# Shifted groups projected as one, and transposed q and k kept in tiles of four blocks

## The chip, the cores and the metric

The kernel runs on one core of a Trainium2 chip. The metric is the device time of one execution in microseconds; a time given for a kernel is the median of its runs.

## The reference, cut to what matters

One encoder block over 2048 tokens of 1024 channels. The input is normalised and projected once; of the projection, mixer A has 8 query heads over 2 heads of keys and values with a window of 128, and mixer B has three groups of 8 heads, each with its own window and dilation. In a dilated group the sequence falls into residue classes, and each class is a short sequence of its own with a window of 64 entries to both sides:

```python
B_GROUPS = ((128, 1), (512, 4), (2048, 16))
...
def dilated_group(q, k, v, window, dilation, bias_table):
    bsz, S, H, dh = q.shape
    L = S // dilation
...
    out, lse = banded_attention(to_sub(q), to_sub(k), to_sub(v), window // (2 * dilation),
                                dilation, bias_table, None)
```

Inside, q and k are normalised per head, logits get a bias by relative position, and everything outside of the window is masked. The three groups of B are then joined by their softmax denominators, both mixers are gated, projected, merged and projected again.

## The kernel before

**Units.** The attention is worked through in 14 units, `unit_order()`: two of A (4 query heads each) and twelve of B, two heads each, for four pairs of heads and three groups g. A unit of group 0 has one class of 16 blocks of 128 tokens, one of group 1 has 4 classes of 4 blocks, one of group 2 has 16 classes of one block. So every unit has 16 blocks, which it takes in eight pairs (`Pair`); 14 x 8 = 112 pairs are the clock of the schedule.

**Split numbers.** Activations and weights are kept as two 16-bit halves, `XH` and `XL`, `wh` and `wl`; a product is three matmuls (high by high, high by low, low by high) over 8 chunks of channels, 24 for a block, added up in one bank.

**Shifted units.** In groups 0 and 1 (`un.shift`) a query block of 128 needs 64 keys to both sides. So k and v of a block are projected from tokens shifted by 64 (`subset(..., aligned=False)`), while q is projected from the block as it stands. Block c of k and v then holds the last 64 tokens of block c-1 and the first 64 of block c; block 0 holds the last 64 of its class and the first 64. A query block reads two such blocks. `matmuls` (L642) writes 24 matmuls of 128 columns for q and 24 of 256 for k and v, into one bank `pj` of which there are two. Units of A and of group 2 have one run of 24 with 384 columns.

**From projection to transposed q and k.** `Pair.plan` places what follows by offsets from the moment a block's projection ends: `evac_qk` (L670) copies q and k to `rw` on ACT; `v_hi` (L685) and `v_lo` (L691) take v on ACT and DVE and so free the bank; then norms (`square`, `stats`, `newton`, `scale`, `gain`), the split into halves `spl` (`hi`, `lo`, `swap`), and `turn` (L741). `turn` issues one DMA transpose for each of the two blocks from SP, into a tile `kq` of its own, [128, 6, 128], of which there are six, or `kq0` for the first block of a shifted class, of which there are three (the last query block of a class needs that one again).

**Items.** A query block is an `Item`, in A one for each two heads. Its `plan` places logits (L792 on, matmuls at L803), maxima with bias (L818, DVE), exponentials (ACT), the split and the DMA transpose of the probabilities (L841, SP) and, some 1.8 pairs later, the product with the values (L852). Logits come three matmuls for each of its key blocks and head, 64 rows each, the two heads in the two halves of the array; each block has its own 128 (at the ends 64) columns of a bank `s`. There are three such banks and an item takes two. Items of a pair p come about 0.77 of a pair after that pair's `turn`.

**What sets the order.** Every step is put by `at(time, ...)` on a heap, and `until(time)` hands out what is due; the order on each engine is therefore written down by hand, and the times are in units of a pair. The projection's own matmuls are handed out evenly by their count: at the k-th of n the clock of the schedule stands at `pos + share * k / n`, and whatever is due then is put in between. The same stream has fills (`g_step`, `mg_step`: gate projections in matmuls of 512 columns, L308). Engines work in order, and SP is the one queue for all DMAs: weights, transposes, `z` out to memory and back, gates.

After the units come the gates, the branch products and the output product (L308, L1407, L1612), which the change doesn't touch.

Of the kernel before, what the change touches and what calls it, by code (L numbers as in the profile page):

```python
# [22 lines left out]
F16 = mybir.dt.float16  # L23
# [10 lines left out]
NCH = D // 128  # L34
# [67 lines left out]
T_OUT = (0.1, 0.1, 1.431, 2.0)  # L102
FILLS = ((2, None, (2, 2, 4, 5)), (3, 0, (8, 9, 10, 12)), (4, 1, (17, 18, 20, 21)), (5, 2, (24, 25, 26, 28)), (6, 3, (32, 35, 37, 38)), (7, 4, (40, 41, 42, 44)), (9, 6, (57, 59, 60, 61)), (10, 7, (64, 65, 66, 68)), (11, 10, (88, 89, 90, 92)), (8, 13, (116, 116, 118, 118)))
XT_BUFS = 14
KQ_BUFS = 6
VT_BUFS = 10
PT_BUFS = 4
N_BIAS_A = 384
# [3 lines left out]
def block_kernel(tc, x, w_units, w_gate, w_mrg, w_brn, w_out, w_bra, gain, qkg, sink, bias_a, bias_b, b_merge, out):  # L112
    nc = tc.nc
# [3 lines left out]
    T = nc.tensor  # L117
# [394 lines left out]
    def scale_time(t):  # L512
        return X_CH[0] + X_CH[1] * t
# [6 lines left out]
    for t in range(NT):  # L520
        b = X_SQ[0] + X_SQ[1] * t if t < 4 else X_SQ[2] + X_SQ[3] * (t - 4)
# [4 lines left out]
        b = scale_time(t)  # L526
        at(b, x_scale, t)
        for h in range(2):
            b = scale_time(t) + X_CH[2] + X_CH[5] * h
# [8 lines left out]
    for c in range(3):  # L538
        b = X_G[c]
# [34 lines left out]
    wk = main.enter_context(tc.tile_pool(name="wk", bufs=2, reuse_waits="tile"))  # L574
# [3 lines left out]
    def xclass(X, g, r):  # L578
        return X[:].rearrange("p c (j d) -> p c d j", d=DIL[g])[:, :, r, :]

    class Unit:


        def __init__(self, u):
            self.kind, self.idx, self.g = UNITS[u]
            self.u = u
            assert ("w", u) in done
            self.wh, self.wl = wtiles[u][3:5]
            if self.kind == "A":
                self.nq, self.nk, self.nv = 4, 1, 1  # L590
                self.d, self.n = 1, NT
            else:
                self.nq, self.nk, self.nv = 2, 2, 2
                self.d = DIL[self.g]
                self.n = S // self.d // 128
            self.br = 0 if self.kind == "A" else 1
            self.shift = self.kind == "B" and self.n > 1
            self.v, self.kq, self.t, self.done = {}, {}, {}, {}
            if self.kind == "A" or self.g == 0:
                self.nm = us.tile([128, NT, self.nq], F32, name=f"nm{self.kind}", bufs=2)  # L600

# [28 lines left out]
    def subset(X, g, r, c, aligned):  # L630
        o = 128 * c if aligned else (128 * c or S // DIL[g]) - 64
        return xclass((XH, XL)[X], g, r)[:, :, o:o + 128]

    class Pair:
# [7 lines left out]
        def matmuls(self, i):  # L642
            un, (r, c) = self.un, self.subsets[i]
            self.ps[i] = ps = pj_p.tile([128, 512], F32, name="pj")
            out = []
            for a, b, aligned in ((0, 128, True), (128, 384, False)) if un.shift else ((0, 384, True),):
                h, lo = subset(0, un.g, r, c, aligned), subset(1, un.g, r, c, aligned)
                k = 0
                for ch in range(NCH):
                    for lhs, rhs in ((h, un.wh), (h, un.wl), (lo, un.wh)):  # L650
                        out.append(lambda lhs=lhs, rhs=rhs, ch=ch, a=a, b=b, k=k: T.matmul(  # L651
                            ps[:, a:b], lhsT=lhs[:, ch, :], rhs=rhs[:, ch, a:b], start=(k == 0), stop=(k == 23)))
                        k += 1
            return out

        def plan(self, e):
# [82 lines left out]
                    G.tensor_copy(self.sp[:, i, :, 5, :], self.sp[:, i, :, 4, :])  # L739

        def turn(self):  # L741
            for i, s in enumerate(self.subsets):
                if self.un.shift and s[1] == 0:
                    kq = wk.tile([128, 6, 128], F16, name="kq0", bufs=3)
                else:
                    kq = wk.tile([128, 6, 128], F16, name="kq", bufs=KQ_BUFS)
                nc.sync.dma_start_transpose(out=kq[:, :self.nw, :], in_=self.sp[:, i].rearrange("p a b c -> p (a b c)"))
                self.un.kq[s] = kq


    class Item:
        def __init__(self, un, r, i, h0):
            self.un, self.r, self.i, self.h0 = un, r, i, h0
            n = un.n
            self.p0 = 0
            if un.kind == "A":
                cs = [c for c in (i - 1, i, i + 1) if 0 <= c < n]
                self.keys = [((0, c), 0, 128) for c in cs]
                self.b0 = 128 * (cs[0] - i + 1)
            elif n == 1:  # L760
                cs = [0]
                self.keys = [((r, 0), 0, 128)]
                self.b0 = 64
            else:
                cs = [i, (i + 1) % n]
                self.keys = [((r, i), 0 if i else 64, 128), ((r, (i + 1) % n), 0, 128 if i + 1 < n else 64)]
                self.b0 = self.p0 = 0 if i else 64
            self.segs = [(r, c) for c in cs]
            self.W = sum(b - a for _, a, b in self.keys)
            self.width = 128 * len(cs)  # L770

        def plan(self, s):
# [18 lines left out]

        def logits(self):  # L792
            un = self.un
            q = un.kq[(self.r, self.i)]
            self.sv = [s_p.tile([128, 512], F32, name="s")[:, :self.W] for _ in range(2)]
            nb = 3 if un.kind == "A" else 2
            o = 0
            for s, k0, k1 in self.keys:
                kt = un.kq[s]
                for i, (a, b) in enumerate(((0, 0), (0, 1), (1, 0))):  # L800
                    for j in range(2):
                        rows = slice(64 * j, 64 * j + 64)
                        T.matmul(self.sv[j][:, o:o + k1 - k0], lhsT=q[rows, nb * a + (self.h0 + j) // 2, :],  # L803
                                 rhs=kt[rows, nb * b + nb - 1, k0:k1], start=(i == 0), stop=(i == 2))
                o += k1 - k0

        def stat(self, j):
            un = self.un
# [251 lines left out]
    for u in range(NU + 1):  # L1060
        t = 8 * u
# [8 lines left out]
    for c, u, slots in FILLS:  # L1070
# [4 lines left out]
        t = 8 * u  # L1075
# [5 lines left out]
    for k in range(8):  # L1081
        u = 3 + k
        t = 8 * u
# [10 lines left out]
    un, nxt = None, 0.0  # L1094
    t = 0
    while t < NPAIR or heap or any(k >= t for k in fill):
        u, j = divmod(t, 8)
        steps = [(f, args) for f, *args in fill.pop(t, [])]
        if u < NU:
            if j == 0:  # L1100
                un = Unit(u)
# [341 lines left out]
    t = clock[0]  # L1443
# [120 lines left out]
    t = clock[0]  # L1564
# [7 lines left out]
    for k, (i, q) in enumerate(steps):  # L1572
# [3 lines left out]
        p = (i // 2, q % 2)  # L1576
# [168 lines left out]
```

## Time and profile before

| | us |
|---|---|
| median of 3 runs | 1980.72 (1979.74 to 1981.89) |
| the profiled execution | 1981.32 |
| its span, first to last instruction | 1979.5 |
| TensorE busy | 1963.7 |
| VectorE (DVE) busy | 1376.8 |
| ScalarE (ACT) busy | 1061.1 |
| GpSimd (POOL) busy | 875.6 |
| projection matmuls of the units, L651, first to last start | 79.9 to 1397.4 |

Busy times are the union of an engine's instructions. PE is TensorE, PEld its weight loads, SP the queue that issues DMAs; a line such as L651 is a line of the kernel. In rows of groups, "out<-in" are the program's tiles, then come partitions x elements of out and in, the count, and behind the bar the busy us and the mean ns of one. A PE row's end is modelled, so its start says more than its length. Rows of the timeline begin with the start in us and the length in us. Rows of windows give length, then for each engine busy us and count, the granted clock of TensorE, the share of the DMA engines and GB/s.

### The profile page before, as it was taken

Reading aid. Unit: us, or ns where it says so; the run is one execution under the profiler, and the core shown is the slowest. Engines: PE = TensorE matmul, PEld = TensorE weight load, DVE = VectorE, ACT = ScalarE, POOL = GpSimd, SP = SyncE. Lnnn points to the kernel's source line nnn. Section 1 sums busy time; section 2 is a strip of 40 time slices with the busy share of each in tenths; the row PEclk is TensorE's granted clock in tenths of the full one; section 3 lists DMA queues with packets and bytes.
Section 4 is the critical chain, followed back from the end, with each engine's and each line's share of the span. In section 5 each row is a group of like instructions: output and inputs, shape, how many; then the busy total and the mean of one; then the engine's idle time right before and its main releaser. Section 6 shows DMA issues by size and latency. Waiting matters only on the chain.

```text
span 1979.5 us, 49754 instructions
## 1 busy us (share of the span) xinstructions
PE 1963.7 (99%) x18614; PEld 1351.0 (68%) x18614; DVE 1376.8 (70%) x3604; ACT 1061.1 (54%) x2415; POOL 875.6 (44%) x2248
## 2 busy tenths in 40 slices
PE   8999999999999999999999999999999999999999
PEld 5557785677878888777888878888544444444444
DVE  6668776888767776667776778767867656776422
ACT  7457655766555566565566655656534545432200
POOL 4254445444445645446454565545520220232533
PEclk9999999999999999999999999999999999999999
DMA  6249976896848585466756675645731355788764
GB/s 248 80 86 171 186 141 142 141 187 129 172 82 176 105 167 114 104 135 149 134 128 131 122 148 118 132 102 102 163 98 55 118 175 182 219 241 271 251 222 153
DMA packets 540626, 295.98 MB, mean 150 GB/s; under 512 B 408928, under 2 KB 478176, under 8 KB 539104
## 3 DMA queue, kind: packets, MB, share of 16 engines
q1 hardware_dynamic: 540384, 292.81, 63.2%
q8 instruction: 145, 2.38, 0.5%
q14 instruction: 97, 0.79, 0.1%
HBM read 129.91 MB, written 65.27 MB: 99 GB/s over the span
## 4 chain that ended last, share of the span: by engine, by line
PE 93%; DVE 3%; POOL 2%; issue 1%; ACT 1%; DMA 0%; SPq 0%; DVEq 0%; POOLq 0%; ACTq 0%
PE pj L651 42%; PE pj L308 15%; PE fps L308 13%; PE fps L1612 7%; PE s L803 5%; PE fps L1407 5%; PE pv L852 4%; PE pt L914 1%; PE s L468 1%; POOL rs_t L270 0%; DMA xt<-in_x_dram 0%; DVE rw L717 0%; POOL rs_t L271 0%; POOL rs_t L272 0%; DVE qss L705 0%
## 5 line engine op out<-in xcount | busy, mean ns | idle before, releaser
L651 PE MATMUL pj<-wl,XH 128*128 128x128 f16 (+2 forms) x2816 | 717.7, 269 | 0.0
L651 PE MATMUL pj<-wh,XL 128*128 128x128 f16 (+2 forms) x2816 | 713.2, 269 | 0.0
L651 PE MATMUL pj<-wh,XH 128*128 128x128 f16 (+2 forms) x2816 | 708.6, 268 | 2.2 <-DVE vt L691 2.2
L651 PEld LDWEIGHTS <-XH 128*128 128x128 f16 x5632 | 575.3, 113 | 71.0 <-issue 2.6
L651 PEld LDWEIGHTS <-XL 128*128 128x128 f16 x2816 | 318.6, 113 | 37.8 <-issue 0.2
L270 POOL TENSOR_TENSOR rs_t<-rs_y 128x8 f32<-128x8 f32 (+2 forms) x345 | 101.2, 293 | 395.0 <-DVE rs_y L261 292.7
L818 DVE CUSTOM_DVE_ANT_0 pr<-s,b,ubuf 128x256 f32<-128x256 f32 (+3 forms) x512 | 219.2, 465 | 80.3 <-PE s L803 78.7
L835 DVE SCALAR_TENSOR_TENSOR p<-pr,p 128x512 f16<-128x512 f32 (+2 forms) x256 | 184.2, 720 | 24.7 <-ACT p L831 24.2
L670 ACT ACTIVATE rw<-pj 128x256 f32<-128x256 f32 (+1 forms) x224 | 86.9, 388 | 201.9 <-PE pj L651 199.8
L308 PEld LDWEIGHTS <-wh 128*128 128x128 f16 x960 | 93.7, 98 | 111.5 <-issue 1.4
L724 POOL TENSOR_TENSOR rw<-rw,g 128x128 f32<-128x128 f32 (+1 forms) x224 | 130.9, 603 | 85.9 <-DVE rw L717 53.3
L831 ACT ACTIVATE p<-pr 128x512 f16<-128x512 f32 (+2 forms) x256 | 159.5, 623 | 6.8
L308 PE MATMUL fps<-Y,wh 128*128 128x512 f16 x512 | 152.3, 379 | 0.0
L308 PE MATMUL pj<-XH,gh 128*128 128x512 f16 x384 | 146.0, 380 | 0.0
L308 PE MATMUL pj<-XH,gl 128*128 128x512 f16 x384 | 145.5, 379 | 0.0
L308 PE MATMUL pj<-XL,gh 128*128 128x512 f16 x384 | 145.5, 379 | 0.0
L1612 PE MATMUL fps<-wt,M 128*128 128x512 f16 (+1 forms) x684 | 145.2, 375 | 0.0
L717 DVE TENSOR_TENSOR rw<-rw,qr 128x512 f32<-128x512 f32 (+1 forms) x112 | 108.4, 968 | 50.1 <-POOL vt L678 33.7
L852 PEld LDWEIGHTS <-pt 128*128 128x128 f16 x3024 | 122.2, 97 | 22.1 <-DMA pt<-p 0.3
L180 POOL TENSOR_TENSOR wraw<-wraw,gn 128x768 f32<-128x768 f32 (+1 forms) x80 | 113.4, 1425 | 43.2 <-DMA wraw<-in_w_mrg_dram 29.5
L852 PE MATMUL pv<-vt,pt 128*128 128x65 f16 (+1 forms) x2784 | 131.7, 193 | 0.0
L803 PEld LDWEIGHTS <-kq 64*128 64x128 f16 x3024 | 82.9, 94 | 69.7 <-issue 65.8
(241 smaller groups left out, 3534.2 us busy)
## 6 DMA issues: line engine op xcount, KB each, us to landing
wraw<-in_w_units_dram SPq DMA_DIRECT2D x56, 384.0 KB, 4.7
mtd<-mm SPq DMA_DIRECT2D x56, 256.0 KB, 3.9
M<-mtd SPq DMA_DIRECT2D x8, 1792.0 KB, 9.0
mgd<-fg SPq DMA_DIRECT2D x39, 256.0 KB, 2.1
zd<-z SPq DMA_DIRECT2D x128, 66.0 KB, 1.8
zz<-zd SPq DMA_DIRECT2D x64, 132.0 KB, 2.8
xt<-in_x_dram SPq DMA_DIRECT2D x16, 512.0 KB, 8.6
gtd<-yo SPq DMA_DIRECT2D x32, 256.0 KB, 3.1
```

Of the source, the lines that this page charges most:

```text
L180: G.tensor_tensor(v, v, gn[:, c0:c0 + 2].unsqueeze(2).to_broadcast([128, 2, n]), OP.mult)
L270: G.tensor_tensor(tv, yv, yv, OP.mult)
L308: out.append(lambda w=w, xx=xx, ch=ch, i=i: T.matmul(ps[:], lhsT=w[:, ch, c0:c0 + 128], rhs=xx[:, ch, ts], start=(i == 0), stop=(i == n - 1)))
L651: out.append(lambda lhs=lhs, rhs=rhs, ch=ch, a=a, b=b, k=k: T.matmul(ps[:, a:b], lhsT=lhs[:, ch, :], rhs=rhs[:, ch, a:b], start=(k == 0), ...
L717: V.tensor_tensor(q, q, self.rr[:, :n].unsqueeze(2).to_broadcast([128, n, HD]), OP.mult)
L724: G.tensor_tensor(q[:, i, :un.nq, :], q[:, i, :un.nq, :], g, OP.mult)
L803: T.matmul(self.sv[j][:, o:o + k1 - k0], lhsT=q[rows, nb * a + (self.h0 + j) // 2, :], rhs=kt[rows, nb * b + nb - 1, k0:k1], start=(i == 0 ...
L818: V.tensor_tensor_reduce(out=self.pv[:, j, self.p0:self.p0 + W], in0=self.sv[j], in1=un.bias[:, self.h0 + j, self.b0:self.b0 + W], scale=I ...
L831: A.activation(self.sp[:, :128 * n], self.pr, AF.Copy, scale=PSC)
L835: V.scalar_tensor_tensor(self.sp[:, 128 * n:], self.pr, PSC, self.sp[:, :128 * n], OP.mult, OP.subtract)
L852: T.matmul(self.po[:, j, :w], lhsT=p[:, n * j + s, :], rhs=un.v[key][:, vh, c0:c0 + w], start=(k == 0 and s == 0), stop=(k == 2 and s == n ...
L1612: mm.append(lambda ch=ch, k=k, w=w, i=i: T.matmul(ps[:, :cols.stop - cols.start], lhsT=m[:, a, ch, k, :], rhs=wt[w][:, b, ch, cols], start ...
```

## The change

q of a shifted unit is projected from the shifted tokens too, together with k and v: one run of 24 matmuls with 384 columns. Transposed q and k then stand in tiles of 2048 columns, of which there are three. In a shifted unit a tile takes four blocks in the order of the tokens: four rows (`a`) of 512 columns, and block b of the shifted kind goes to columns 128 b - 64 to 128 b + 64. The block in which a tile begins is therefore transposed in two halves of 64 rows, one to the end of the tile before (or, for the first block of a class, to the end of the class's own tile) and one to the start of the new one. In group 0, whose class has four tiles, the first and last 64 tokens of the class that belong to query block 15 go to a small tile `kqe`, which takes a third transpose in the last pair. In units of A and of group 2 a tile takes the two blocks of a pair.

An item's q is then one stretch of 128 columns, and its keys are one or two stretches of 64, 128, 192 or 256 columns, as far as they lie side by side in one tile; each stretch is one set of three matmuls for each head.

```diff
 XT_BUFS = 14
-KQ_BUFS = 6
+KQ_BUFS = 3
 VT_BUFS = 10
...
             self.shift = self.kind == "B" and self.n > 1
-            self.v, self.kq, self.t, self.done = {}, {}, {}, {}
+            self.v, self.kq, self.kt, self.t = {}, {}, {}, {}
             if self.kind == "A" or self.g == 0:
...
             out = []
-            for a, b, aligned in ((0, 128, True), (128, 384, False)) if un.shift else ((0, 384, True),):
-                h, lo = subset(0, un.g, r, c, aligned), subset(1, un.g, r, c, aligned)
-                k = 0
-                for ch in range(NCH):
-                    for lhs, rhs in ((h, un.wh), (h, un.wl), (lo, un.wh)):
-                        out.append(lambda lhs=lhs, rhs=rhs, ch=ch, a=a, b=b, k=k: T.matmul(
-                            ps[:, a:b], lhsT=lhs[:, ch, :], rhs=rhs[:, ch, a:b], start=(k == 0), stop=(k == 23)))
-                        k += 1
+            h, lo = subset(0, un.g, r, c, not un.shift), subset(1, un.g, r, c, not un.shift)
+            k = 0
+            for ch in range(NCH):
+                for lhs, rhs in ((h, un.wh), (h, un.wl), (lo, un.wh)):
+                    out.append(lambda lhs=lhs, rhs=rhs, ch=ch, k=k: T.matmul(
+                        ps[:, :384], lhsT=lhs[:, ch, :], rhs=rhs[:, ch, :384], start=(k == 0), stop=(k == 23)))
+                    k += 1
             return out
...
         def turn(self):
-            for i, s in enumerate(self.subsets):
-                if self.un.shift and s[1] == 0:
-                    kq = wk.tile([128, 6, 128], F16, name="kq0", bufs=3)
+            un, nw = self.un, self.nw
+            def turned(out, i, rows=slice(0, 128)):
+                nc.sync.dma_start_transpose(out=out, in_=self.sp[rows, i].rearrange("p a b c -> p (a b c)"))
+            if not un.shift:
+                t = wk.tile([128, 2048], F16, name="kq", bufs=KQ_BUFS)[:, :256 * nw].rearrange("p (a b) -> p a b", a=nw)
+                for i, s in enumerate(self.subsets):
+                    turned(t[:, :, 128 * i:128 * i + 128], i)
+                    un.kq[s] = t, 128 * i
+                return
+            for i, (r, c) in enumerate(self.subsets):
+                m, b = divmod(un.n * r + c, 4)
+                if b == 0:
+                    un.kt[m] = wk.tile([128, 2048], F16, name="kq", bufs=KQ_BUFS)[:].rearrange("p (a b) -> p a b", a=4)
+                    if c == 0 and un.n > 4:
+                        un.ke = wk.tile([128, 4, 128], F16, name="kqe", bufs=1)
+                        turned(un.ke[:, :, 64:128], i, slice(0, 64))
+                    else:
+                        turned(un.kt[m if c == 0 else m - 1][:, :, 448:512], i, slice(0, 64))
+                    turned(un.kt[m][:, :, 0:64], i, slice(64, 128))
                 else:
-                    kq = wk.tile([128, 6, 128], F16, name="kq", bufs=KQ_BUFS)
-                nc.sync.dma_start_transpose(out=kq[:, :self.nw, :], in_=self.sp[:, i].rearrange("p a b c -> p (a b c)"))
-                self.un.kq[s] = kq
+                    turned(un.kt[m][:, :, 128 * b - 64:128 * b + 64], i)
+                if c == un.n - 1 and un.n > 4:
+                    turned(un.ke[:, :, 0:64], i, slice(64, 128))
 
...
                 cs = [c for c in (i - 1, i, i + 1) if 0 <= c < n]
-                self.keys = [((0, c), 0, 128) for c in cs]
+                self.W = 128 * len(cs)
                 self.b0 = 128 * (cs[0] - i + 1)
...
                 cs = [0]
-                self.keys = [((r, 0), 0, 128)]
+                self.W = 128
                 self.b0 = 64
...
                 cs = [i, (i + 1) % n]
-                self.keys = [((r, i), 0 if i else 64, 128), ((r, (i + 1) % n), 0, 128 if i + 1 < n else 64)]
+                self.W = 256 if 0 < i < n - 1 else 192
                 self.b0 = self.p0 = 0 if i else 64
             self.segs = [(r, c) for c in cs]
-            self.W = sum(b - a for _, a, b in self.keys)
             self.width = 128 * len(cs)
...
             un = self.un
-            q = un.kq[(self.r, self.i)]
+            q, keys = self.operands()
             self.sv = [s_p.tile([128, 512], F32, name="s")[:, :self.W] for _ in range(2)]
...
             o = 0
-            for s, k0, k1 in self.keys:
-                kt = un.kq[s]
+            for kt, k0, w in keys:
                 for i, (a, b) in enumerate(((0, 0), (0, 1), (1, 0))):
...
                         rows = slice(64 * j, 64 * j + 64)
-                        T.matmul(self.sv[j][:, o:o + k1 - k0], lhsT=q[rows, nb * a + (self.h0 + j) // 2, :],
-                                 rhs=kt[rows, nb * b + nb - 1, k0:k1], start=(i == 0), stop=(i == 2))
-                o += k1 - k0
+                        T.matmul(self.sv[j][:, o:o + w], lhsT=q[0][rows, nb * a + (self.h0 + j) // 2, q[1]:q[1] + 128],
+                                 rhs=kt[rows, nb * b + nb - 1, k0:k0 + w], start=(i == 0), stop=(i == 2))
+                o += w
+            assert o == self.W
+        def operands(self):
+            un, r, i, n = self.un, self.r, self.i, self.un.n
+            if not un.shift:
+                keys = []
+                for s in self.segs:
+                    t, o = un.kq[s]
+                    if keys and keys[-1][0] is t:
+                        keys[-1] = t, keys[-1][1], keys[-1][2] + 128
+                    else:
+                        keys.append((t, o, 128))
+                return un.kq[r, i], keys
+            m, b = divmod(n * r + i, 4)
+            t = un.kt[m]
+            q = (t, 128 * b) if i < 15 else (un.ke, 0)
+            if b == 0:
+                return q, ([(un.kt[m - 1], 448, 64)] if i else []) + [(t, 0, 192)]
+            if b < 3:
+                return q, [(t, 128 * b - 64, 256)]
+            if i == 15:
+                return q, [(t, 320, 128), (un.ke, 64, 64)]
+            return q, [(t, 320, 192)] + ([(un.kt[m + 1], 0, 64)] if i < n - 1 else [])
 
...
             un = self.un
```

## The prediction

> **What bounds the kernel now.** I read the page first: header, slices, chain.
>
> ```profile
> span 1979.5 us, 49754 instructions
> PE 1963.7 (99%) x18614; PEld 1351.0 (68%) x18614; DVE 1376.8 (70%) x3604; ACT 1061.1 (54%) x2415; POOL 875.6 (44%) x2248
> PE   8999999999999999999999999999999999999999
> ...
> PEclk9999999999999999999999999999999999999999
> ...
> PE 93%; DVE 3%; POOL 2%; issue 1%; ACT 1%; DMA 0%; SPq 0%; DVEq 0%; POOLq 0%; ACTq 0%
> ```
>
> TensorE is occupied in every slice, at the full granted clock, and 93% of the chain that ended last is its own work. DVE, ACT and POOL have a third or more of the span to spare. So whatever shortens TensorE's own stream shortens the run, as long as no other engine makes it wait. It hardly waits now, as the view of waits kept to TensorE says:
>
> ```profile
> PE pj L651 <- DVE vt L691: 2.2, 2, 1.8
> PE s L803 <- DVE nmB L818: 1.4, 1, 1.4
> ```
>
> (Columns: total us, times, longest us; the larger rows belong to the opening.) A busy TensorE isn't yet one that can go faster, because the durations of matmuls overlap. What counts is the distance from start to start, which the timeline shows. First the last stage, where one line runs unbroken (columns: start, us, instruction, count):
>
> ```profile
> 1839.67 40.52 PE L1612 MATMUL fps<-wt,M 128*128 128x512 f16 x187
> ...
> 1973.49 2.78 PE L1612 MATMUL fps<-wt,M 128*128 128x256 f16 x24
> ...
> L1612 PE MATMUL fps<-wt,M 128*128 128x512 f16 x660 | 142.6, 379 | 0.0
> ...
> L1612 PE MATMUL fps<-wt,M 128*128 128x256 f16 x24 | 2.8, 273 | 0.0
> ```
>
> The last two rows are of the groups by shape (busy us, mean ns of one): a matmul itself lasts 379 ns at 512 columns and 273 ns at 256. So 512 columns take (40.52 - 0.38)/186 = 215.8 ns from start to start, 256 take (2.78 - 0.27)/23 = 109.1 ns. The difference gives 0.417 ns a column, and what is left at no columns is 109.1 - 106.7 = **2.4 ns for each matmul, whatever its width**. By that line 128 columns should take 55.8 ns and 384 columns 162.5 ns. The line that the change edits agrees, in three unbroken stretches (24 rows of 128 and of 256, 29 of 384, first and next or last shown):
>
> ```profile
> 1201.44 0.22 PE L651 MATMUL pj<-wh,XH 128*128 128x128 f16 x1
> ...
> 1202.78 0.27 PE L651 MATMUL pj<-wh,XH 128*128 128x256 f16 x1
> ...
> 1208.11 0.27 PE L651 MATMUL pj<-wh,XH 128*128 128x256 f16 x1
> ...
> 1210.72 0.38 PE L308 MATMUL pj<-XH,gh 128*128 128x512 f16 x1
> ...
> 116.55 0.33 PE L651 MATMUL pj<-wh,XL 128*128 128x384 f16 x1
> ...
> 121.10 0.33 PE L651 MATMUL pj<-wh,XH 128*128 128x384 f16 x1
> ```
>
> 1.34/24 = 55.8 ns, 2.61/24 = 108.8 ns, 4.55/28 = 162.5 ns.
>
> **The change part by part.** *Projection of shifted groups.* Eight of the 14 units are shifted, 16 blocks each, 128 blocks. By shape, the groups of L651 are (one of three equal rows each, busy us and mean ns behind the bar):
>
> ```profile
> L651 PE MATMUL pj<-wh,XL 128*128 128x256 f16 x1024 | 280.9, 274 | 0.0
> ...
> L651 PE MATMUL pj<-wh,XL 128*128 128x384 f16 x768 | 252.5, 329 | 0.0
> L651 PE MATMUL pj<-wh,XL 128*128 128x128 f16 x1024 | 184.9, 220 | 0.0
> ```
>
> So 3 x 1024 = 3072 pairs (128 and 256 columns) become 3072 matmuls of 384. The columns stay; the fixed part goes once per pair: 3072 x 2.4 ns = 7.4 us. From the three stretches alone it is 55.8 + 108.8 - 162.5 = 2.1 ns, 6.5 us; with 109.1 for 256 it is 2.4. I take **-7.4**, bounds -6.5 and -8. That 3072 weight loads go too (113 ns each on the page) is worth nothing beyond this: at 55.8 ns from start to start they already lie beneath other matmuls.
>
> The Trainium skill speaks of the same spacing twice. TensorE: Matmul & The Clock Gate, under "Wait — 56ns, not 53.3ns?", has a fixed cost of about 2.5 ns per warm matmul, which by itself would make 7.7 us; the trace agrees with 2.4. The same page, under "Back-to-back issue gap", says that real streams of load and matmul sustain about 81 ns at 128 columns and 131 ns at 512; a straight line through these has 64 ns at no columns, and the sum would be 3072 x 64 ns = 197 us. The 55.8 and 215.8 ns above disagree with it.
>
> *Logits.* Keys that lie side by side in a tile go through in one matmul. From the code: in the 64 items of A six fewer each, in the 64 of group 1 six fewer, in group 0 nine of 16 items per unit have six fewer: 64x6 + 64x6 + 4x9x6 = 984 of 3024. Two heads run side by side, so 492 starts go. Rows of 18 and 12 such matmuls:
>
> ```profile
> 201.08 0.68 PE L803 MATMUL s<-kq 64*128 64x128 f16 x18
> ...
> 1140.85 0.51 PE L803 MATMUL s<-kq 64*128 64x128 f16 x12
> ```
>
> 0.17 us for three pairs of 128 columns is 57 ns a pair, the same 55.8 within the rounding. At 2.4 ns: **-1.2 us**, bounds 0 and -1.5. The number of times TensorE enters and leaves the 64-row form stays (256 items, each one group).
>
> *Transposes.* They are issued by SP:
>
> ```profile
> L747 SPq DMA_TRANSPOSE kq<-spl x224: 1188/1238/2262, 100.1 to 1416.2; - x112
> ...
>   PEld L803: 0.3, 1
> ...
> DMA to landing us min/median/max: 2.4/2.9/5.9
> ```
>
> Where a tile of four begins, the block is turned in two halves: one issue more in 16 classes of group 1 and 16 tiles of group 0, plus one at the end of each of four group 0 units: 36 more, 36 x 1.24 = 45 us of SP's time, beside TensorE. SP is in order: behind an extra issue wait the other k and q of the pair, the transposes of probabilities, z and weight loads. Half-height transposes into strided columns aren't in this trace; the nearest row bounds one at 1.19 us (the shortest issue) and 2.26 (the longest), and I take 1.24, as the issue time hardly depends on anything here. Only one load of logits ever waited for a landing (0.3 us), so there is slack; who has least of it? The logits that come first after a pair's turn:
>
> ```profile
> 1124.64 2.50 SPq L747 DMA_TRANSPOSE kq<-spl  x2
> DMA to landing us min/median/max: 2.5/2.8/3.1
> ...
> 1129.13 0.51 PE L803 MATMUL s<-kq 64*128 64x128 f16 x12
> ...
> 1404.07 2.50 SPq L747 DMA_TRANSPOSE kq<-spl  x2
> DMA to landing us min/median/max: 3.9/4.1/4.4
> ...
> 1408.85 0.34 PE L803 MATMUL s<-kq 64*128 64x128 f16 x6
> ```
>
> (The landing rows are those of the two issues above each.) In the third unit of group 0 the first of the pair landed 3.1 us after 1124.64 at the latest, 1.4 us ahead of 1129.13. In the last unit it landed by 4.4 us after 1404.07, 0.4 us ahead of 1408.85. Both are pairs at which a tile begins, so these logits now need the second issue, 1.24 us later. The first still has 0.1 to 0.2 us; the second is late by 0.9, and TensorE stands for it, with the fills queued behind.
>
> *Where logits stand between projections.* The interleaving counts matmuls. So far the first 24 of 48 were the short ones and took a third of a block's time; now time and count agree. A group written at half a block therefore comes up to a sixth of a block later, 24 x 162.5/6 = 0.65 us, in a shifted unit. At 1408.85 only fills are left, which stay as they are, and the up to four blocks between the pair's first eviction and these logits are shorter, 4 x 24 x 2.4 ns = 0.2 us, which makes the 0.9 above about **+1.1 us**. Later logits are later for DVE, whose maxima wait for them already, and behind these stand the evictions (L691) that free the projection's banks; those have a whole block, 3.9 us, so 0.65 us at the most is covered. Where that cover is gone, the two waits shown at the start are what it looks like. They came at one place:
>
> ```profile
> 1135.58 0.49 PE L803 MATMUL s<-kq 64*128 64x128 f16 x11 [1.36 <-DVE nmB L818]
> ...
> 1146.00:1154.00 8.00, 6.15 (x62) 5.13 (x60) 7.69 (x29) 4.65 (x14) 2.85 (x13) 0.79 0.84 186
> ```
>
> DVE was full there (7.69 of 8 us, third column of pairs) and the granted clock fell to a mean of 0.79 in the 8 us after the second wait, that is 8 x 0.21 = 1.7 us lost on top of 1.4 + 1.8: 4.9 us in all. The order on DVE isn't changed, so I leave it as it is: 0, bounds -4.9 (gone) and +4.9 (a second one like it).
>
> The Trainium skill speaks against the tiles: DMA: Bandwidth & Descriptors, in the row "DMA_TRANSPOSE effective BW", gives about 30% less where the middle dimension isn't contiguous, as now. By that the 2.9 us to landing would be 3.8 at most, the last unit would wait some 1.5 us more, and the sum would be -6.0. No row of this trace shows a strided one.
>
> *Sum.* -7.4 - 1.2 + 1.1 = **-7.5 us**. The profiled execution took 1981.3 us, 1.8 of it around its span of 1979.5; the median of the runs shown is 1980.7. From the median: 1973.2 us. Own range: -8.0 - 1.5 = -9.5, and -6.5 + 2.3 (the last unit late by 2.26 instead of 1.24, logits at nothing) = -4.2, so 1971.2 to 1976.5.
>
> **The rivals.** *The waits of DVE go as well.* Logits that come 0.2 us and more later give the second bank of scores more time. For it: one such place in a span. Against it: DVE, not TensorE, was late there. Time: 1973.2 - 4.9 = 1968.3.
>
> *DVE sets the pace in part.* Group 0 units have the merging of the three groups on DVE beside all else. If TensorE gained nothing in them (4 of 8 shifted units, 3.7 us) or one more stall of 4.9 us came: 1976.9 to 1978.1. For it: the full DVE above. Against it: 70% of the span.
>
> *The extra issues lie on the path (slower).* Place: the first logits after each of the 36 tiles' beginnings. Price: 1.24 us each, 44.6 us if all are late, 1980.7 - 8.6 + 44.6 = 2016.7. It decides from 8.6/1.24 = 7 of them being late in full. For it: two places have under 1.5 us. Against it: the 0.3 us in 3024 loads of logits.
>
> *Weight loads set the pace.* If every matmul had to last as long as its load of 113 ns, a pair cost 226 and one of 384 costs 162.5: 63 ns x 3072 = 195 us, 1785 us. The skill's 81 ns would give nearly the same. The row of 55.8 ns is against it.
>
> **How the numbers follow.** Runs of this kernel lie within 0.1% of each other; what it can tell from no change is about 0.2%, 4 us, so faster ends at 1976.8. Forecast 0.58; DVE's waits gone 0.14; DVE in part 0.18, two thirds of it above 1976.8; extra issues on the path 0.09, of which 0.05 beyond 1984.7 and 0.04 with a few late, within 0.2%; weight loads 0.01. Faster: 0.58 + 0.14 + 0.06 + 0.01 = 0.79. Same: 0.12 + 0.04 = 0.16. Slower: 0.05. The range takes in the rivals of DVE on both sides, 1968.3 and 1978.1, with a us beside each: 1967 to 1979.
>
> **What would show it.** L651's matmuls all at 384 columns, 5376, at 162.5 ns; L803's at 2040; its share of the time before 1400 shorter by 8 us, the last 500 us unchanged. Wrong: waits of TensorE for kq in more than two places; a longer row of waits for DVE in group 0; landings of kq far above 2.9 us; or the end of the projections (1397 us now) not some 7 us earlier.

## The result and the profile after

| | before | changed | ratio, 95% interval |
|---|---|---|---|
| median at first (7 runs each) | 1979.83 us | 1973.91 us | 0.9969, 0.9957 to 0.9980 |
| median once more (15 and 5 runs) | 1980.47 us | 1974.04 us | 0.9969, 0.9956 to 0.9981 |
| span of the profiled execution | 1979.5 us | 1971.7 us | |

Some 6 us by the medians (the ratio, 0.0031, is 6.1 us), 7.8 by the two spans; why these differ is seen below. The page of the changed kernel has, where the prediction showed these lines of before:

```profile
span 1971.7 us, 41743 instructions
PE 1952.1 (99%) x14558; PEld 1166.2 (59%) x14558; DVE 1374.9 (70%) x3604; ACT 1063.9 (54%) x2415; POOL 876.2 (44%) x2248
...
PE 90%; DVE 4%; POOL 2%; issue 1%; DMA 1%; ACT 1%; SPq 0%; DVEq 0%; POOLq 0%; ACTq 0%
```

The other engines do what they did, with the same counts; TensorE has 4056 matmuls fewer, 3072 of the projection and 984 of the logits, and is still what ends last. Its spacing at the edited line, in a shifted unit (first row of an unbroken stretch of 16, and what follows):

```profile
1200.12 0.33 PE L650 MATMUL pj<-wh,XL 128*128 128x384 f16 x1
...
1202.72 0.38 PE L308 MATMUL pj<-XH,gh 128*128 128x512 f16 x1
```

2.60/16 = 162.5 ns, as forecast for 384 columns. Where the time went, from two windows of each kernel, up to the end of the units' projections and after it (length first; then PE's busy time):

```profile
79.00:1397.50 1318.50, 1314.93 (x15348) 1039.78 (x15347) 968.74 (x2817) 798.16 (x1965) 681.87 (x2036) 1.00 0.68 134
1397.50:1979.50 582.00, 577.47 (x2862) 266.48 (x2859) 350.10 (x648) 208.99 (x357) 165.71 (x155) 1.00 0.58 181
```

```profile
79.00:1388.00 1309.00, 1304.18 (x11311) 855.02 (x11310) 968.13 (x2817) 801.19 (x1965) 681.70 (x2035) 1.00 0.65 135
1388.00:1971.70 583.70, 577.53 (x2843) 266.08 (x2841) 348.73 (x648) 208.77 (x358) 166.44 (x156) 1.00 0.58 181
```

The first stretch is 9.5 us shorter, the second 1.7 longer. TensorE's waits, from the view of waits of the changed kernel (total us, times, longest):

```profile
PE pj L650 <- DVE vt L690: 2.7, 2, 2.4
PE s L818 <- DVE nmB L857: 2.0, 1, 2.0
...
PE s L818 <- DMA kq<-spl: 0.7, 1, 0.7
PE pt L953 <- DVE ya L1054: 0.6, 1, 0.6
```

The two waits for DVE are those of before, 2.2 and 1.4 us then, each about half a us longer. The last two are new and lie in the second stretch: 1.3 of its 1.7 us. One more row is of the weight loads of the logits, where the kernel before had a single wait of 0.3 us:

```profile
PEld L818 <- DMA kq<-spl: 2.5, 5, 1.2
```

Five loads now waited for a transpose; only the longest of these waits held the matmuls up, by the 0.7 us above. The granted clock differs too. Around the wait for L690:

```profile
1139.50:1147.50 8.00, 5.63 (x39) 3.59 (x38) 7.72 (x28) 4.45 (x13) 2.62 (x13) 1.00 0.64 150
```

At this place the kernel before had a mean of 0.79 over 8 us. Here it is 1.00 although the wait was longer (the last section shows what decides this). So 1.7 of the 7.8 us between the spans are a stretch of half clock that one execution had and the other didn't.

### The profile page after: what moved, and what is told of

It is laid out like the page before. It is cut to its first block, busy times and chain, and to the rows that moved or that the text cites. A ratio compares the mean times of both kernels' runs of the same rounds, so it can differ in the third digit from the quotient of the medians.

```text
span 1971.7 us, 41743 instructions
## 1 busy us (share of the span) xinstructions
PE 1952.1 (99%) x14558; PEld 1166.2 (59%) x14558; DVE 1374.9 (70%) x3604; ACT 1063.9 (54%) x2415; POOL 876.2 (44%) x2248
## 4 chain that ended last, share of the span: by engine, by line
PE 90%; DVE 4%; POOL 2%; issue 1%; DMA 1%; ACT 1%; SPq 0%; DVEq 0%; POOLq 0%; ACTq 0%
PE pj L650 41%; PE pj L308 14%; PE fps L308 13%; PE fps L1651 7%; PE s L818 5%; PE fps L1446 5%; PE pv L891 4%; PE pt L953 1%; PE s L468 1%; POOL rs_t L270 1%; DVE rw L716 1%; POOL rs_t L271 0%; DMA xt<-in_x_dram 0%; DVE qss L704 0%; DVE p L874 0%
## 5 line engine op out<-in xcount | busy, mean ns | idle before, releaser
L650 PE MATMUL pj<-wl,XH 128*128 128x384 f16 x1792 | 589.6, 329 | 0.0
L650 PE MATMUL pj<-wh,XH 128*128 128x384 f16 x1792 | 584.6, 326 | 2.7 <-DVE vt L690 2.7
L650 PE MATMUL pj<-wh,XL 128*128 128x384 f16 x1792 | 586.4, 327 | 0.0
L650 PEld LDWEIGHTS <-XH 128*128 128x128 f16 x3584 | 412.0, 117 | 177.3 <-issue 23.6
L650 PEld LDWEIGHTS <-XL 128*128 128x128 f16 x1792 | 209.5, 117 | 69.4 <-issue 2.1
L818 PE MATMUL s<-kq 64*128 64x256 f16 (+2 forms) x1992 | 123.1, 242 | 2.7 <-DVE nmB L857 2.0
```

The lines of the kernel that those rows point to most:

```text
L650: out.append(lambda lhs=lhs, rhs=rhs, ch=ch, k=k: T.matmul(ps[:, :384], lhsT=lhs[:, ch, :], rhs=rhs[:, ch, :384], start=(k == 0), stop=(k ...
L818: T.matmul(self.sv[j][:, o:o + w], lhsT=q[0][rows, nb * a + (self.h0 + j) // 2, q[1]:q[1] + 128], rhs=kt[rows, nb * b + nb - 1, k0:k0 + w] ...
```

## The experiments

All are edits of the changed kernel, except the last.

**Two parts and three parts.** The projection alone, cut again, from the same shifted tokens:

```diff
-            k = 0
-            for ch in range(NCH):
...
-                        ps[:, :384], lhsT=lhs[:, ch, :], rhs=rhs[:, ch, :384], start=(k == 0), stop=(k == 23)))
+            for a, b in ((0, 128), (128, 384)) if un.shift else ((0, 384),):
+                k = 0
...
+                            ps[:, a:b], lhsT=lhs[:, ch, :], rhs=rhs[:, ch, a:b], start=(k == 0), stop=(k == 23)))
```

and with `((0, 128), (128, 256), (256, 384))`.

> The changed kernel with the projection of shifted blocks again in 24 matmuls of 128 columns and then 24 of 256, from the same shifted tokens; tiles, transposes and logits as changed. Theory A (each matmul has a fixed 2.4 ns, and 3072 fewer of them are the gain): 3072 x 2.4 = 7.4 us more, some 1 us of it swallowed where TensorE waits for DVE in the third unit of group 0: 1973.9 + 6.4 to 7.4 = 1980.3 to 1981.3. Rival B (the gain is in the logits, the tiles, or waits that moved): within 2 us of 1973.9.

> The same projection in three parts of 128 columns, 72 matmuls a block, 6144 more than changed. Theory A: 6144 x 2.4 = 14.7 us more, 1987 to 1989, twice the step of two parts; starts 55.8 ns apart. Rival C (weight loads set the pace below some width, 113 ns a load in the groups): 72 loads a block instead of 24, far more than twice the step of two parts, up to 6144 x 113 ns = 694 us.

Two parts: 1981.88 us, ratio to before 1.0006 (0.9996 to 1.0015), that is 0.0037 above the changed kernel's 0.9969, 7.3 us (the median itself lies above the range expected, as does the median of the kernel before beside it, 1981.05 us). Three parts: 1987.86 us, 1.0040 (1.0025 to 1.0055), 0.0071 or 14 us above it. So 3072 matmuls more cost 7.3 us and 6144 cost 14: 2.4 and 2.3 ns each. By the intervals these differences are good to about 3 and 4 us, an estimate, so the clock alone gives 2.4 ns only to within 1 ns; the starts below give it closer. In three parts (66 starts between the first and the last row):

```profile
1147.23 0.22 PE L651 MATMUL pj<-wh,XH 128*128 128x128 f16 x1
...
1150.91 0.22 PE L651 MATMUL pj<-wh,XH 128*128 128x128 f16 x1
```

3.68/66 = 55.8 ns with a weight load for each. Loads don't set the pace; rival C and the prediction's last rival are out. Two parts are as slow as the kernel before although their logits are the wide ones, so rival B is out as well.

**Keys by 128.**

```diff
+            keys = [(kt, k0 + i, min(128, w - i)) for kt, k0, w in keys for i in range(0, w, 128)]
             for kt, k0, w in keys:
```

> The changed kernel with its logits' keys cut into at most 128 columns again: 3024 matmuls for 2040. Theory A: 492 pairs x 2.4 ns = 1.2 us more, 1975.1; a group of 12 lasts 441 ns to the next matmul instead of 434 of 6 wide ones. Rival B (logits carry the gain): 1979 or more.

1976.94 us, 0.9981 (0.9972 to 0.9990): 0.0012 or 2.4 us above the changed kernel. The expectation miscounted: in 24 items of group 0 keys of 192 and 64 columns now become three pieces, not two, which makes 3168 matmuls for the logits. The count of all matmuls says so too, 1128 more than the changed kernel's 14558:

```profile
PE 1954.9 (99%) x15686; PEld 1186.0 (60%) x15686; DVE 1375.4 (70%) x3604; ACT 1064.4 (54%) x2415; POOL 877.7 (44%) x2248
```

That is 564 pairs, and theory A's price is 1.4 us; it lies within what the two intervals allow, and so does no difference at all. Rival B's 1979 isn't reached. The profiled execution also has a stretch of half clock (window; the granted clock is the third figure from the end) and waits 0.8 us longer for a transpose (view of waits):

```profile
1127.00:1135.00 8.00, 6.03 (x52) 3.30 (x51) 7.62 (x23) 5.73 (x15) 4.86 (x13) 0.79 0.86 199
```

```profile
PE s L819 <- DMA kq<-spl: 1.5, 1, 1.5
```

How much is due to the matmuls themselves shows in the starts. Changed kernel, a group of six with 256 columns and what follows; before, a group of twelve with 128:

```profile
1256.06 0.50 PE L818 MATMUL s<-kq 64*128 64x256 f16 x6
1256.49 0.38 PE L650 MATMUL pj<-wl,XH 128*128 128x384 f16 x1
```

```profile
1140.85 0.51 PE L803 MATMUL s<-kq 64*128 64x128 f16 x12
1141.29 0.28 PE L651 MATMUL pj<-wh,XL 128*128 128x256 f16 x1
```

0.43 against 0.44 us is at the rounding of the view, but the traces hold starts to 1 ns and there are many such groups. From a group's first start to the next projection matmul, in the mean of all that no wait interrupts: 434.0 ns for six wide ones (58 groups of the changed kernel) against 441.3 ns for twelve (58 groups with keys by 128); in A 601.3 against 608.8 ns (38 groups each). Each saves 7.3 to 7.5 ns for three pairs, 2.4 to 2.5 ns a pair. For 492 pairs that is the 1.2 us of the prediction, shown by the starts where the clock can't resolve it.

**More transposes.**

```diff
                 if b == 0:
+                    turned(wk.tile([128, 4, 64], F16, name="kqx", bufs=2)[:], i, slice(0, 64))
```

> The changed kernel with one half-height transpose more (into a tile that nobody reads) ahead of the others wherever a tile of four begins: 32 more issues of SP. Theory A (extra issues lie beside TensorE, but for the last unit): 32 x 1.24 = 40 us more of SP, the wait in the last unit longer by 1.2 us, one or two new ones of under 1 us each: 1975 to 1977. Rival P (extra issues lie on the path): 10 to 40 us more, 1984 to 2014.

1974.05 us, 0.9970 (0.9960 to 0.9980): no different from the changed kernel, and a us below what theory A forecast. Rival P's 10 us and more are out. The extra issues aren't free, though: with 32 more (first view, by line) TensorE's wait in the last unit is longer by 1.0 us in the profiled execution, and ten loads of logits wait, 5.0 us in all, for five and 2.5 us (view of waits). The other nine stay hidden.

```profile
L744 SPq DMA_TRANSPOSE kqx<-spl x32: 1169/1171/1686, 216.5 to 1395.3; - x32
```

```profile
PE s L819 <- DMA kq<-spl: 1.7, 1, 1.7
...
PEld L819 <- DMA kq<-spl: 5.0, 10, 2.2
```

**The wide part first.** Two parts in the order `((128, 384), (0, 128))`.

> The two-part projection with its order turned round: 24 matmuls of 256 columns (k and v) and then 24 of 128 (q). As many matmuls as with the narrow part first; only the place of logits and values between the projections moves, which is at 0.77 of a block by count: at 0.70 of its time with the narrow part first, at 0.77 undivided, at 0.85 here. Theory A (the count of matmuls is what costs, the place doesn't): the same as the two-part kernel within 1.5 us, ratio to before 1.000 to 1.002. Rival D (the place of logits made the gain or a loss): 2 us or more away from it.

1981.73 us, 1.0009 (0.9999 to 1.0018), the two-part kernel's within 0.6 us. Where logits stand between the projections is worth nothing that shows here; the two intervals together leave room for some 2.5 us, so rival D's 2 us aren't seen, though not shut out to the last us.

**The preparation of a gate chunk.** Both waits for DVE lie in the third unit of group 0. In the changed kernel, DVE's short operations ahead of the maxima there, and POOL beside them (timelines):

```profile
1126.82 0.41 DVE L1029 TENSOR_TENSOR bm_n<-zz 128x4 f32<-128x4 f32 x1
1127.26 0.97 DVE L1030 TENSOR_TENSOR bm_n<-bm_n,zz 128x4 f32<-128x4 f32 x1
1128.26 1.02 DVE L1031 TENSOR_TENSOR bm_e<-bm_n,zz 128x12 f32<-128x12 f32 x1
1129.20 0.47 DVE L857 CUSTOM_DVE_ANT_0 pr<-s,b,ubuf 128x256 f32<-128x256 f32 x1
...
1127.17 1.03 POOL L324 TENSOR_TENSOR wraw<-wraw,gn 128x512 f32<-128x512 f32 x1
1128.15 0.10 POOL L677 MEMSET vt<- 128x2 f16 x1
1128.20 1.03 POOL L324 TENSOR_TENSOR wraw<-wraw,gn 128x512 f32<-128x512 f32 x1
```

4 columns take DVE 0.97 us and end when POOL's operation ends. L324 belongs to the weights of gate chunk 11, which this unit prepares.

```diff
-(11, 10, (88, 89, 90, 92))
+(11, 9, (88, 89, 90, 92))
```

> The changed kernel with the weights of one gate chunk (fill 11: gain L324 on POOL, square, split L354 on DVE) prepared one unit earlier, in the group 2 unit ahead of the third group 0 unit; its fills stay where they are. Theory E (TensorE waits there for DVE because this preparation falls into it: POOL's gain of 1.03 us twice beside DVE's short operations, which take 0.97 and 1.02 us instead of 0.17, and L354's 1.28 us ahead of an eviction): waits for L857 and L690 of 2.0 and 2.4 us go, 4 to 5 us less, 1969 to 1970. Rival F (DVE is too full in a group 0 unit without fills, whatever is prepared): the waits stay within 1 us, 1973 to 1974.

> The changed kernel once more, beside the two that follow: 5 to 8 us below the kernel before (ratio 0.996 to 0.9975).

> The kernel with the preparation of chunk 11 moved one unit ahead, once more. Theory E: 3 to 5 us below the changed kernel of this call, ratio to before 0.994 to 0.9955.

At first 1970.34 us, 0.9953 (0.9938 to 0.9968); once more, beside the changed kernel's repetition, 1970.44 us, 0.9951 (0.9937 to 0.9964) against 0.9969 (0.9956 to 0.9981). That is 3.6 us below the changed kernel by the medians, and the best version here. DVE's operations and TensorE's waits in the second run:

```profile
1127.19 0.17 DVE L1030 TENSOR_TENSOR bm_n<-bm_n,zz 128x4 f32<-128x4 f32 x1
1127.39 0.18 DVE L1031 TENSOR_TENSOR bm_e<-bm_n,zz 128x12 f32<-128x12 f32 x1
```

```profile
PE pj L650 <- DVE vt L690: 1.6, 2, 1.2
...
PE s L818 <- DVE nmB L857: 0.5, 1, 0.5
```

0.17 and 0.18 us, and 1.6 + 0.5 of waiting instead of 2.7 + 2.0. Theory E has the cause of a little over half of the waits, 2.6 us, and the gain of 3.6 us stays short of the 4 to 5 it forecast; the other waits stay with the unit. The edit takes POOL's gain and DVE's own L354 out of the unit together, so their shares aren't separated.

**Fills in that unit, and later logits.**

```diff
-(11, 10, (88, 89, 90, 92))
+(11, 9, (82, 84, 85, 87))
...
-                nxt = max(nxt, t + LS)
+                nxt = max(nxt, t + LS + (.2 if u == NU - 1 else 0))
```

> As the kernel before it in this call, and the four fills of this chunk go into the third group 0 unit (pairs 82, 84, 85, 87) instead of the next unit, so that TensorE has 5.2 us more to do in four of its pairs. Theory E: nothing more to win, 1969 to 1970. Rival F: only now the waits go, 4 us or more below the kernel before it.

> As the one before, and the logits of the last unit are placed 0.2 of a pair (1.6 us) later. If the wait for the second half of a transposed block in the last unit (0.7 us in the changed kernel) is worth its length, 0.7 us less; waits for kq gone. If the later logits only push the end of the unit, 0 to 2 us more.

Both miss. With the fills moved: 1980.61 us, 1.0004 (0.9995 to 1.0014), 10 us above the kernel without. The unit that lost the fills now waits for DVE (in the last row, the longer of the two; the shorter is the changed kernel's):

```profile
PE s L818 <- DVE nmB L857: 4.0, 2, 3.7
PE s L818 <- DVE z L857: 1.9, 1, 1.9
PE pt L953 <- DVE ya L1054: 1.6, 2, 1.1
```

With later logits in the last unit too: 1989.23 us, 1.0049 (1.0034 to 1.0064). The wait for kq is gone, as forecast, but the waits for DVE grew, four for the maxima and two for L690, where the run before had two and one (of 0.3 us). What these two rows grew by, 3.6 us, lies in the last unit; the rest of the 9 us isn't traced here:

```profile
PE s L818 <- DVE nmB L857: 5.6, 4, 3.7
PE pj L650 <- DVE vt L690: 2.3, 2, 2.0
```

**The kernel before, with the preparation moved.** The edit of `FILLS` above, on the kernel before.

> The kernel before with the same preparation moved one unit ahead: the undivided change is then measured on a schedule with less waiting for DVE. Theory E: its waits for L818 and L691 in the third group 0 unit (1.4 and 1.8 us) shrink by 2 us or more and with them the stretch of half clock that followed: 2 to 4 us below before, 1976 to 1978. Theory A: the step from it to the kernel of 384 columns with the same move is 7 to 8 us, a little more than the step between the two unmoved kernels, as less of it goes to DVE. Rival: the step is the same or smaller.

1977.36 us, 0.9988 (0.9979 to 0.9996). Its wait for L691 is 1.2 us in all and that for the maxima's bank is gone, as theory E has it. From it to the best version the ratio falls by 0.0037, 7.3 us; between the unmoved two it falls by 0.0031, 6.1 us. That is theory A's direction, but the intervals overlap, so whether the change gives back a us to DVE's waits stays open by the clock; only the waits themselves show it (3.6 us before, 4.7 after; with the preparation moved 1.2 and 2.1).

## Why the prediction was right

1973.2 us was forecast, 1973.9 measured, and the mechanism is the one forecast. That the number is so close is in part luck: the forecast starts from the median of three runs, 1980.7, where that of seven is 1979.8. The step was to be 7.5 us and is 6.1 by the ratio. The spans say 7.8, but with the 1.7 of half clock, 6.1 again. The terms as they came out add up to it: -7.4 for the projection, -1.2 for the logits, +0.7 for a transpose, +1.1 for the two old waits for DVE, +0.6 for a new one (L1054) = -6.2 us.

- **Projection, -7.4.** Right in mechanism and size: 162.5 ns at 384 columns, and 7.3 us between the two-part kernel and the changed one.
- **Logits, -1.2.** Right by the starts, 7.3 to 7.5 ns a group; by the clock only consistent.
- **Transposes, +1.1.** A wait of 0.7 us in the last unit, but not the one that was worked out. In the pair that was named the first landings now took 3.0 us at most where they had taken 4.4, and its logits (1399.92) didn't wait. The wait came one pair later, for a transpose of full height:

```profile
1395.14 3.77 SPq L744 DMA_TRANSPOSE kq<-spl  x3
...
1399.92 0.51 PE L818 MATMUL s<-kq 64*128 64x192 f16 x12
...
1403.62 0.44 SPq L175 DMA_DIRECT2D wraw<-in_w_mrg_dram  x1
1404.17 1.76 SPq L880 DMA_TRANSPOSE pt<-p  x1
1406.08 3.26 SPq L744 DMA_TRANSPOSE kq<-spl  x2
...
1411.16 0.50 PE L818 MATMUL s<-kq 64*128 64x256 f16 x6 [0.73 <-DMA kq<-spl]
```

  The landings of these three and of these two `kq` issues (view of the line, each in its window), and below them those of the same last two in the kernel before:

```profile
DMA to landing us min/median/max: 2.4/2.5/3.0
...
DMA to landing us min/median/max: 4.0/4.5/5.0
```

```profile
DMA to landing us min/median/max: 2.5/2.6/2.7
```

  So the cause is a landing of 5.0 us. The issue in halves may still stand behind it. In the kernel before the same issues of SP are:

```profile
1404.07 2.50 SPq L747 DMA_TRANSPOSE kq<-spl  x2
...
1411.68 0.48 SPq L175 DMA_DIRECT2D wraw<-in_w_mrg_dram  x1
1412.27 2.55 SPq L841 DMA_TRANSPOSE pt<-p  x1
1415.01 2.50 SPq L747 DMA_TRANSPOSE kq<-spl  x2
```

  In both, the last two begin 10.94 us after the pair ahead of them. But the third issue there pushes the weight load and the transposed probabilities back, so that these begin 2.5 and 1.9 us ahead of the last two instead of 3.3 and 2.7. How much of the 5.0 us is due to that traffic, and how much to anything else in the new tiles, no run separates.

- **The page against the tiles.** The Trainium skill (DMA: Bandwidth & Descriptors, "DMA_TRANSPOSE effective BW") has about 30% less bandwidth for a middle dimension that isn't contiguous. (The prediction put 30% on the time; 30% less bandwidth would make 2.9 us into 4.1, not 3.8.) All landings here took 2.3 to 6.1 us, 2.6 in the median, against 2.4 to 5.9 and 2.9 before. In the units of A and of group 2, where a block is still one transpose, the medians are 2.8 and 2.7 us, against 2.8 and 2.9 before. No loss shows at this size.
- **DVE's waits, put at 0.** This is the term that was off. They came again and longer, 2.0 and 2.4 us for 1.4 and 1.8, and L1054 added 0.6. A longer row of waits for DVE in group 0 was one of the prediction's own signs of being wrong. It came, at about a fifth of the 4.9 us that the rival of DVE was priced at. That DVE had a third of the span to spare was also a little much: it is 30%, and around these two waits it was busy for 14.3 of 16 us. What was mis-sized is the half clock: the prediction put 1.7 us with these waits as one price of 4.9, and in the changed kernel the waits came without it.
- **Place of the logits, 0.** Nothing shows against it, as the wide part first has it.

## What to carry to other kernels

On a stream that TensorE alone bounds, count its instructions as well as its columns: take the start-to-start time at two widths, draw the line, and what is left at no columns (2.4 ns here) is the worth of each matmul that a merge removes. Before trusting a shorter stream, look for the places where it already waits for an engine that isn't the bound on average; moving one preparation out of such a place was worth 3.6 us, a little over half of the 6.1 that the whole merge gave. Fills of matmuls can be what lets that engine keep up, so moving them moves the waits.

## What the runs showed of the hardware

- DVE's operations on 4 and 12 columns took 0.97 and 1.02 us beside POOL's operations of 1.03 us and 0.17 and 0.18 us without them, in otherwise the same place. Of the 32 such operations of 4 columns (`bm_n<-bm_n,zz`) in the changed kernel two took 0.97 us, both beside an operation of L324; the other 30 took 0.16 to 0.21. One engine's short work can last as long as the other's long one.
- After a wait of about 2 us TensorE's granted clock was halved for 3.4 us in some executions and not in others. The kernel before waited 1.85 us and was halved 1.2 us later (first two rows: the matmul that ended the wait, and the window with its clock of 0.50); the changed one waited 2.37 us and kept its clock:

```profile
1149.16 0.22 PE L651 MATMUL pj<-wh,XH 128*128 128x128 f16 x1 [1.85 <-DVE vt L691]
...
1150.40:1153.80 3.40, 3.40 (x27) 2.67 (x22) 3.26 (x15) 1.13 (x3) 2.53 (x11) 0.50 0.84 218
```

```profile
1143.34 0.32 PE L650 MATMUL pj<-wh,XH 128*128 128x384 f16 x1 [2.37 <-DVE vt L690]
```

  What decides, as far as the traces here show, is where a wait falls. In each of them the granted clock changes only at multiples of 3.413 us from one another (in the kernel before, 1122.98 us or 329 steps lie between two changes). Cut into such windows, between the opening and the end, TensorE's idle time was followed by half clock in the next window where it came to 1.85 us (kernel before), 1.88 (two parts), 1.89 and 2.16 (fills moved), 1.93 (more transposes), 1.96, 2.19 and 2.27 (later logits) and 1.97 (keys by 128). It was not where it came to 1.82 us or less: of the 2.37 us above, 1.61 fell into one window and the rest into the next, and in the changed kernel's repetition 1.82 and 1.76 us of waits of 2.04 and 2.38 fell into one. The one exception is a window with 1.42 us that was itself at half clock (later logits). So here 1.85 us of idle time in one window were enough and 1.82 weren't, a little over half of it (the last digit is soft, as the ends of matmuls are modelled), and the same wait can cost nothing or a halved window.
- A halved window loses 3.41/2 = 1.7 us, over a quarter of this change, if no wait follows. With more transposes it came ahead of the wait for L690, which then was 0.9 us long instead of 2.4, so most of the loss was given back.
- The Trainium skill (TensorE: Matmul & The Clock Gate, "What's actually happening") has a window of 3413 ns that runs freely, and half rate after at least one idle window. The length agrees with the 3.41 us here. If that means a window idle as a whole, it wasn't needed here: 1.85 us of it were enough.
